# Layer 1's sparse-attention indexer with a narrow key projection and chunk-wise first products, the last norm by token halves, and one DMA sum fewer in the first unit

## The chip, the core and the metric

One core of one Trainium2 chip runs the whole program in one launch. The metric is the device time of the program in microseconds (us): the median of the runs shown. TensorE (PE in the rows) does the matrix products, VectorE (DVE), ScalarE (ACT) and GpSimd (POOL) the elementwise work, SyncE (SP) starts most loads.

## What is computed

The reference takes x, 512 tokens of 1024 features, through two layers, each of a half-step feed-forward, a mixer and another half-step feed-forward, all in fp32. The feed-forwards are SwiGLU with 2816 hidden features behind an RMS norm. Layer 0's mixer is a pair of state-space and mLSTM heads, which the change does not touch. Layer 1's mixer is sparse attention: an indexer scores each query against the keys, the 256 best of them stay, and attention runs on those. Cut to that:

```
q, k, v, qi, ki, wi = split(rms_norm(x) @ w_in)    # 1024 | 64 | 64 | 512 | 64 | 8 columns
q  = rope(rms_norm(q, 16 heads of 64));  k = rope(rms_norm(k))
qi = rope(qi, 8 heads of 64);            ki = rope(ki)
logits = einsum('thd,sd->tsh', qi, ki)
score  = einsum('tsh,th->ts', relu(logits), wi) * scale, -inf where s > t
sel    = top_k(score, 256)
o = softmax(q . k[sel] / 8, causal) @ v[sel];      x = x + o @ w_out
```

The first 128 tokens have at most 128 keys each, fewer than 256: of them only the index key ki is needed, not qi and wi.

## The kernel before, in words

**Products.** Every fp32 product is made of three matmuls: each operand is split into a high and a low part, and `mm3` (lines 276 to 282) adds high x high (L280), high x low (L281) and low x high (L282) into one PSUM bank. x lies in SBUF as 8 chunks of 128 features x 512 tokens. Ahead of a stage it is multiplied by the norm's gain and split into `xgn`: high part on ScalarE (L767), low part on VectorE (L770). The norm's scale by token, `rcol`, is applied only after the product, when ScalarE copies a bank out. `prep_later` does this for two chunks at a time; it also squares each chunk (ScalarE, L781) and adds the squares up (GpSimd, L476) into the tile `ssq`. The squares of the last two chunks are not added but stay separate summands. `settle_later` then has TensorE sum the squares over the features with one-column matmuls (`sums`, L411 to L415: 4 token blocks, each over all summands), VectorE scale and shift the result (L743), and GpSimd raise it to the power -1/2 (L745). A feed-forward also needs the scale along the rows: four transposes (`rows_of`, L435) and a copy (L749).

**Weights.** A weight block is loaded by SyncE into one of the 4 buffers `raw`, in turn, and formed into high and low parts in one of two ways (`both`). The plain way is `parts`: ScalarE copies the high part (L481) and VectorE subtracts for the low part (L483). The *summed* way has ScalarE write -raw (L510), then a DMA issued by GpSimd add raw to it in place (L511), and ScalarE write the high part (L512). For the sum to be the low part, -raw is written in the rounded type, so that adding raw leaves the rounding's rest.

**Order.** The feed-forwards' and the attention's work is entered into a plan: each step with its engine, an estimated duration, what it reads and writes. A list scheduler (`Plan.order`) takes at each point the step that can start earliest by the estimates, among equals the one that is due first, and the instructions of each engine are then pinned in that order. TensorE's steps carry a stream name ("filler", "index", "logits", "values"); within a stream they keep the order in which they were entered. One such plan holds FFN00, a second FFN01, FFN10, the attention and FFN11. Buffers that rotate are part of the plan: the n-th user of a tag with m buffers waits for the user m before it.

**The attention** (`attention`, from L1451). The indexer's weights are 584 columns: 512 of qi, 64 of ki, 8 of wi. They are taken in two halves (g = 0 and 1) of 292 columns, each in three blocks `iw` of chunks 0 to 2, 3 to 5 and 6 to 7, six blocks in all, loaded at L1467 and formed the plain way. So ki and wi lie in half 1. The products are made per token block b of 128 tokens and half g, each [128 tokens x 292], over 8 chunks, in the order (b, g) = (0,0), (1,0), (0,1), (1,1), (2,0), (3,0), (2,1), (3,1), in the two banks `gm` and `po` by turns. After the first product `settle_later` is entered, and from then on ScalarE copies each finished bank to `pr` with the scale (L1502). Then, per token block: rotary positions (`rope`, L1419 to 1423, VectorE), a doubled copy of the key (`twice`), transposes (`turned`), and for b = 1 to 3 the index logits (L1542), relu (L1548), weighted sum on VectorE (L1552, L1555), causal selection on GpSimd (L1557) and the top-k: 16 rounds of MAX8 and MATCH_REPLACE8 (L1760, L1761), which a constant of 60 keeps behind other work for b > 1. Behind the index products on TensorE come the key and value product, the queries (weights loaded at L1573, formed the summed way), then per token block the logits, softmax and values of the heads, in the order heads(0), heads(1), out(0), heads(2), heads(3), out(1, first 4 rows), out(1, last 4 rows). `out(half, ...)` is the output product for 256 tokens; after each chunk it is added to x (L476). In the last call `prep_later` is entered after every second chunk, for FFN11's norm, over all 512 tokens.

**The first unit.** A feed-forward unit has 4 weight blocks: gate and up, each in two interleaved halves (0, 1: gate; 2, 3: up). In the very first unit blocks 0 and 1 are formed the plain way and blocks 2 and 3 the summed way; the number is the last argument at the call in `ffn` (`2 * (1 - u) if first else 4`), where `u` is the unit: all four of unit 1 are summed.

## Time and profile before

| | us |
|---|---|
| median of 3 runs (lowest, highest) | 2037.05 (2032.81, 2038.75) |
| the profiled execution's own time | 2032.47 |
| its span in the profile | 2030.8 |
| mean granted TensorE clock over the span | 0.994 of full speed |
| TensorE busy | 1992.4 (98% of the span) |
| VectorE busy | 1581.0 (78%) |
| ScalarE busy | 1169.7 (58%) |
| GpSimd busy | 264.3 (13%) |

Times in rows count from the span's start. Matmuls are pipelined, so a TensorE row's duration overlaps the next row's; the distance of two starts is what one costs. The granted clock is a share of full speed, and its two levels are 1.00 (2.4 GHz) and 0.50 (1.2 GHz).

### The profile page before, as it was taken

The page shows a single profiled execution, that of the slowest core. Times are in us where ns is not written, and L with a number is a line of the kernel's source. Part 1 is how long each engine was busy: PE and PEld are TensorE (multiplying, and loading weights), DVE is VectorE, ACT ScalarE, POOL GpSimd, SP SyncE. Part 2 cuts the span into 40 slices and gives each one's busy share as a digit, 9 for nine tenths or more (in the row PEclk, how much of TensorE's full clock was granted, in tenths as well). Part 3 has the DMA queues.
Part 4 walks back from the last instruction along what each step waited for, and adds up shares of the span by engine and source line. Part 5 has one row for each costly group of instructions (what it writes and reads, how often), then busy time and mean ns, then how long its engine had stood idle before and what let it go on. Part 6 is the DMA issues. An engine that isn't in the chain of part 4 may idle for free.

```text
span 2030.8 us, 34575 instructions
## 1 busy us (share of the span) xinstructions
PE 1992.4 (98%) x13994; PEld 1808.0 (89%) x13994; DVE 1581.0 (78%) x2332; ACT 1169.7 (58%) x1709; POOL 264.3 (13%) x333
## 2 busy tenths in 40 slices
PE   8999999999999999999999999999998999999998
PEld 6999999887788888999998899999865667999998
DVE  6988888876537648988888998878588747988886
ACT  6666656442335434656566665656667544756565
POOL 1000001310001011010002000000215221101010
PEclk9999999999999999999999999999899999999999
DMA  8566665322221232666555366665653202566664
GB/s 220 143 161 153 167 153 141 115 83 74 72 84 63 74 102 65 167 159 164 156 151 140 99 172 157 167 152 141 175 124 90 63 11 73 148 161 161 155 168 114
DMA packets 211592, 260.74 MB, mean 128 GB/s; under 512 B 13804, under 2 KB 186984, under 8 KB 211432
## 3 DMA queue, kind: packets, MB, share of 16 engines
q1 hardware_dynamic: 190640, 185.58, 29.6%
q0 software_dynamic: 20592, 72.89, 19.1%
q8 instruction: 110, 1.80, 0.4%
q14 instruction: 50, 0.41, 0.1%
q10 hardware_dynamic: 200, 0.06, 0.0%
HBM read 183.53 MB, written 2.10 MB: 91 GB/s over the span
## 4 chain that ended last, share of the span: by engine, by line
PE 90%; DVE 5%; DMA 2%; issue 2%; ACT 1%; POOL 1%; ACTq 0%; DVEq 0%; POOLq 0%; SPq 0%
PE pA L281 10%; PE pA L280 10%; PE pA L282 10%; PE pD L281 5%; PE pD L280 5%; PE pD L282 5%; PE pB L281 3%; PE pB L280 3%; PE pB L282 3%; PE po L280 2%; PE po L282 2%; PE po L281 2%; PE pu L280 2%; PE pu L282 2%; PE ptok L280 1%
## 5 line engine op out<-in xcount | busy, mean ns | idle before, releaser
L483 DVE TENSOR_TENSOR form<-raw,form 128x1024 fp32r<-128x1024 f32 (+1 forms) x326 | 389.1, 1199 | 108.7 <-ACT form L481 107.9
L481 ACT ACTIVATE form<-raw 128x1024 fp32r<-128x1024 f32 (+1 forms) x326 | 333.4, 1027 | 178.8 <-DVE raw L476 129.4
L280 PE MATMUL pA<-xf,form 128*128 128x256 f32 x1152 | 322.2, 280 | 0.0
L281 PE MATMUL pA<-xf,form 128*128 128x256 f32 x1152 | 322.2, 280 | 0.0
L282 PE MATMUL pA<-xf,form 128*128 128x256 f32 x1152 | 322.0, 279 | 0.0
L476 DVE TENSOR_TENSOR raw<-raw 128x1024 f32<-128x1024 f32 (+2 forms) x241 | 283.8, 1181 | 12.7 <-DMA raw<-in_ffn_w_down 5.5
L511 POOL DMA_DIRECT2D form<-raw x137 | 117.9, 860 | 1206.0 <-ACT form L510 1145.9
L510 ACT ACTIVATE form<-raw 128x1024 fp32r<-128x1024 f32 (+1 forms) x137 | 141.3, 1031 | 142.5 <-PE pD L282 76.6
L280 PEld LDWEIGHTS pA<-xf,form 128*128 128x128 f32 x1152 | 216.5, 188 | 0.2
L281 PEld LDWEIGHTS pA<-xf,form 128*128 128x128 f32 x1152 | 216.4, 188 | 0.2
L282 PEld LDWEIGHTS pA<-xf,form 128*128 128x128 f32 x1152 | 216.3, 188 | 0.0
L281 PE MATMUL pA<-hid,form 128*128 128x256 f32 x704 | 198.6, 282 | 1.4 <-DVE hid L483 1.1
L280 PE MATMUL pA<-hid,form 128*128 128x256 f32 x704 | 198.1, 281 | 0.1
L282 PE MATMUL pA<-hid,form 128*128 128x256 f32 x704 | 196.9, 280 | 0.0
L281 PE MATMUL pD<-xf,form 128*128 128x256 f32 x576 | 161.2, 280 | 0.0
L280 PE MATMUL pD<-xf,form 128*128 128x256 f32 x576 | 161.2, 280 | 0.0
L282 PE MATMUL pD<-xf,form 128*128 128x256 f32 x576 | 161.1, 280 | 0.0
L476 DVE TENSOR_TENSOR ft<-ft 128x256 f32<-128x256 f32 (+2 forms) x288 | 146.3, 540 | 4.6 <-ACT ft L729 1.1
L512 ACT ACTIVATE form<-raw 128x1024 fp32r<-128x1024 f32 (+1 forms) x137 | 139.9, 1022 | 0.0
L281 PEld LDWEIGHTS pA<-hid,form 128*128 128x128 f32 x704 | 132.4, 188 | 3.2 <-DVE hid L483 3.1
L280 PEld LDWEIGHTS pA<-hid,form 128*128 128x128 f32 x704 | 132.3, 188 | 0.6 <-DVE ft L476 0.5
L282 PEld LDWEIGHTS pA<-hid,form 128*128 128x128 f32 x704 | 132.1, 188 | 0.0
(443 smaller groups left out, 5210.9 us busy)
## 6 DMA issues: line engine op xcount, KB each, us to landing
form<-raw POOLq DMA_DIRECT2D x121, 512.0 KB, 5.8
raw<-in_ffn_w_gate SPq DMA_DIRECT2D x88, 512.0 KB, 3.8
raw<-in_ffn_w_up SPq DMA_DIRECT2D x88, 512.0 KB, 3.7
raw<-in_ffn_w_down SPq DMA_DIRECT2D x64, 512.0 KB, 4.3
raw<-in_hy_w_in SPq DMA_DIRECT2D x44, 512.0 KB, 3.5
raw<-in_ffn_w_down SPq DMA_DIRECT2D x32, 384.0 KB, 3.4
raw<-in_hy_w_out SPq DMA_DIRECT2D x16, 512.0 KB, 3.3
form<-raw POOLq DMA_DIRECT2D x16, 384.0 KB, 4.1
```

The source lines that it names most:

```text
L280: mm(out, l[0], r[0], start=start, stop=False)
L281: mm(out, l[0], r[1], start=False, stop=False)
L282: mm(out, l[1], r[0], start=False, stop=stop)
L476: (self.p if pool else self.v)(n, lambda: e.tensor_tensor(out(), x(), y(), op=op), reads, writes)
L481: self.s(n, lambda: nc.scalar.activation(hi(), src(), AF.Copy), srck, hik)
L483: n, lambda: nc.vector.tensor_tensor(lo(), src(), hi().bitcast(F32), op=ALU.subtract), srck + hik, lok
L510: self.s(n, lambda: nc.scalar.activation(f()[:, 1], raw, AF.Copy, scale=-1.0), rawk, lok)
L511: self.plan.add("gpsimd", 0.85, lambda: nc.gpsimd.dma_start(f()[:, 1], raw, accum_op=ALU.add), rawk + lok, lok, 5.5)
L512: self.s(n, lambda: nc.scalar.activation(f()[:, 0], raw, AF.Copy), rawk, hik)
```

## The change

Three edits. (1) The indexer: product (0,0) is not made; product (0,1) is made only for the 64 columns of ki. The first four products, (0,1), (1,0), (1,1), (2,0), get a bank each and are made chunk by chunk group: chunks 0 to 3 of all four, then 6 and 7, then 4 and 5. `settle_later` and the four scaled copies come after all four. Then (2,1), (3,0), (3,1) follow one by one. The rotary scratch, the doubled key and the transposed queries share one 8 KB slot (`ri`, 2 buffers), likewise in `prepare` (`rq`, 2 buffers), and `pr` holds two token blocks per tile. (2) FFN11's norm: `prep_later` can do one half of the tokens. Chunks 0 to 3 of half 0 are done after out(0), chunks 0 to 3 of half 1 and chunks 4 to 7 whole after out(1). The squares lie in one tile of four. (3) The first unit forms block 2 the plain way too; only block 3 is summed.

```diff
-    def prep_later(self, which, k, last, squares=True):
+    def prep_later(self, which, k, last, squares=True, half=None):
...
-        if k == 0:
+        if k == 0 and not half:
...
+            squares4 = Lazy(lambda: self.tmp.tile([P, 4, T], F32, name="ssq", tag="ssq", bufs=1))
+            self.sqs = [lambda i=i: squares4()[:, i] for i in range(4)]
...
+        halves = (0, 1) if half is None else (half,)
+        cols = slice(halves[0] * H, halves[-1] * H + H)
+        n = cols.stop - cols.start
...
-                    made = self.unit(raws, stream, bool(first) and not u, 2 * (1 - u) if first else 4)
+                    made = self.unit(raws, stream, bool(first) and not u, 3 * (1 - u) if first else 4)
...
-        for b0 in (0, 2):
-            for g in range(2):
-                for b in (b0, b0 + 1):
-                    ps, psk = self.bank(("gm", "po")[b % 2])
-                    for g2, k, f, fk, j in iw:
...
-                    if self.pending == 2:
-                        self.settle_later()
-                        rcol = self.rcol
+        def indexer(jobs, ks):
+            for b, g, (ps, psk) in jobs:
+                cols = slice(0 if b else KI - N1, N1 if b else KI - N1 + 64)
+                tok = slice(b * P, (b + 1) * P)
+                for k, f, fk, j in ((k, f, fk, j) for k0 in ks for g2, k, f, fk, j in iw if (g2, k) == (g, k0)):
+                    product(
+                        lambda ps=ps, cols=cols: ps()[:, cols], psk, lambda k=k, tok=tok: [xg[i][k][:, tok] for i in range(2)], xgk(k),
+                        lambda f=f, j=j, cols=cols: [f()[:, i, j, cols] for i in range(2)], [(*fk, 0), (*fk, 1)],
+                        cols.stop - cols.start, k == 0, k == 5,
+                    )
...
+        jobs = [(0, 1, self.bank("gm")), (1, 0, self.bank("po")), (1, 1, self.bank("lg")), (2, 0, self.bank("lg"))]
+        for ks in ((0, 1, 2, 3), (6, 7), (4, 5)):
+            indexer(jobs, ks)
+        self.settle_later()
+        rcol = self.rcol
+        scaled(jobs)
+        for b, g, tag in ((2, 1, "gm"), (3, 0, "po"), (3, 1, "gm")):
+            jobs = [(b, g, self.bank(tag))]
+            indexer(jobs, (0, 1, 2, 3, 6, 7, 4, 5))
+            scaled(jobs)
...
+            ri, rik = self.spot("ri", (4 * T,), 2)
+            self.rope(x, xk, n, cos, sin, [tk(0), tk(1)], ri, rik)
...
-                if last and k % 2:
-                    self.prep_later(nxt, k - 1, k == KC - 1)
+                if last and k % 2 and (half or k < 4):
+                    self.prep_later(nxt, k - 1, k == KC - 1, half=half if k < 4 else None)
...
-        out(0, range(KC))
+        out(0, range(KC), True)
```

## Rows read from the trace of the kernel before

**Rows 1.** The page's parts 1 and 4: busy time of each engine (share of the span) and instructions; and the chain of work that ended last, shares of the span by engine.

```profile
PE 1992.4 (98%) x13994; PEld 1808.0 (89%) x13994; DVE 1581.0 (78%) x2332; ACT 1169.7 (58%) x1709; POOL 264.3 (13%) x333
...
PE 90%; DVE 5%; DMA 2%; issue 2%; ACT 1%; POOL 1%; ACTq 0%; DVEq 0%; POOLq 0%; SPq 0%
```

**Rows 2.** One answer of the windows view. Columns: the stretch (us from the span's start), its length; then busy us (instructions) of PE, PEld, DVE, ACT and POOL; the granted TensorE clock as a share of full speed; the busy share of the DMA engines; GB/s. The first three stretches are the indexer's products, the fourth row is the attention from the first top-k round to the last, the last two the start of FFN11.

```profile
1435.20:1440.20 5.00, 2.09 (x12) 1.39 (x11) 4.97 (x6) 4.08 (x8) 2.93 (x3) 1.00 0.01 4
1440.20:1453.80 13.60, 12.87 (x52) 12.18 (x53) 8.71 (x15) 5.23 (x10) 1.22 (x2) 0.50 0.57 176
1453.80:1478.40 24.60, 24.60 (x177) 22.61 (x177) 5.12 (x13) 16.04 (x29) 5.57 (x7) 1.00 0.94 212
...
1484.40:1608.50 124.10, 115.63 (x591) 74.81 (x590) 111.79 (x341) 83.69 (x187) 43.00 (x62) 0.99 0.40 90
...
1664.00:1689.30 25.30, 22.03 (x161) 20.18 (x160) 19.94 (x25) 14.40 (x21) 7.70 (x5) 1.00 0.34 105
1689.30:1696.20 6.90, 6.90 (x23) 5.84 (x23) 0.24 (x2) 0.00 (x0) 1.03 (x1) 0.51 0.00 0
```

**Rows 3.** The timeline of TensorE in the index stage: start us, duration us, engine, line, operation, out<-in, shape, count, and in brackets the idle time before it and what ended it.

```profile
1440.83 0.61 PE L281 MATMUL gm<-iw,xgn 128*128 128x292 f32 x1 [1.53 <-DVE iw L483]
...
1445.30 0.42 PE L414 MATMUL pssq<-raw,ssq 128*128 128x1 f32 x2
...
1450.28 0.59 PE L280 MATMUL po<-iw,xgn 128*128 128x292 f32 x1
...
1454.37 0.30 PE L280 MATMUL po<-iw,xgn 128*128 128x292 f32 x1
...
1454.77 0.30 PE L280 MATMUL po<-iw,xgn 128*128 128x292 f32 x1
```

**Rows 4.** What feeds the index stage, 1428 to 1448: the timelines of VectorE, GpSimd (POOL), ScalarE (ACT) and SyncE's queue (SPq), and last the DMA issues of the same stretch (KB each, median us from issue to landing).

```profile
1430.23 2.16 DVE L483 TENSOR_TENSOR iw<-raw,iw 128x876 fp32r<-128x876 f32 x1
...
1434.01 0.74 DVE L770 SCALAR_TENSOR_TENSOR xgn<-raw,xgn 128x512 fp32r<-128x512 f32 x1
...
1437.26 1.46 DVE L770 SCALAR_TENSOR_TENSOR xgn<-raw,xgn 128x512 fp32r<-128x512 f32 x1
...
1438.64 2.14 DVE L483 TENSOR_TENSOR iw<-raw,iw 128x876 fp32r<-128x876 f32 x1
...
1444.69 2.71 DVE L483 TENSOR_TENSOR iw<-raw,iw 128x876 fp32r<-128x876 f32 x3
...
1436.89 2.96 POOL L476 TENSOR_TENSOR ssq<-ssq,sq 128x512 f32<-128x512 f32 x2 [3.35 <-ACT sq L781]
...
1443.59 0.69 ACT L481 ACTIVATE iw<-raw 128x584 fp32r<-128x584 f32 x1 [0.78 <-DMA raw<-in_sa_w_in]
...
1429.41 11.80 SPq L1467 DMA_DIRECT2D raw<-in_sa_w_in  x3
...
raw<-in_sa_w_in SPq DMA_DIRECT2D x2, 438.0 KB, 3.3
```

**Rows 5.** The timelines of GpSimd, ScalarE and VectorE between the sums and the first rotary operation of token block 1: the power that makes the scale, the first scaled copy out of PSUM, the first rotary product.

```profile
1450.69 1.14 POOL L745 TENSOR_TENSOR raw<-raw 128x4 f32<-128x4 f32 x1 [10.80 <-DVE raw L743]
...
1451.87 0.50 ACT L1502 ACTIVATE pr<-gm,raw 128x292 f32<-128x292 f32 x1 [7.59 <-POOL raw L745]
...
1462.34 0.76 DVE L1419 TENSOR_TENSOR rot<-pr,raw 128x576 f32<-128x576 f32 x1 [2.50 <-ACT pr L1502]
```

**Rows 6.** The instructions on the tile of the scores: the top-k's maxima by shape (mean ns of each), with the first start and the last end.

```profile
L1760 DVE MAX8 keep<-keep x48: 418/555/697, 1484.4 to 1606.6; 128x8 f32<-128x256 f32 x16, 128x8 f32<-128x384 f32 x16, 128x8 f32<-128x512 f32 x16
```

**Rows 7.** The timelines around the starts of FFN11 (first four rows, TensorE and VectorE) and of FFN10 (last two: the first of its sums, and the first matmul behind them).

```profile
1676.19 0.50 PE L281 MATMUL pg<-xgn,form 128*128 128x512 f32 x1 [0.77 <-DVE xgn L770]
...
1680.99 0.50 PE L281 MATMUL pg<-xgn,form 128*128 128x512 f32 x1 [1.42 <-DVE xgn L770]
...
1688.03 0.38 PE L414 MATMUL pssq<-raw,sq 128*128 128x1 f32 x2 [1.00 <-ACT sq L781]
...
1676.39 1.64 DVE L770 SCALAR_TENSOR_TENSOR xgn<-raw,xgn 128x512 fp32r<-128x512 f32 x1
...
1104.83 0.28 PE L414 MATMUL pssq<-raw,ssq 128*128 128x1 f32 x2
...
1107.42 0.48 PE L280 MATMUL pu<-xgn,form 128*128 128x512 f32 x1
```

**Rows 8.** The costliest groups by line and shape: two groups of half-width (256-column) instructions; busy us, mean ns | idle us before them.

```profile
L476 DVE TENSOR_TENSOR ft<-ft 128x256 f32<-128x256 f32 x176 | 68.1, 422 | 2.5
...
L1322 ACT ACTIVATE hsq<-pn 128x256 f32<-128x256 f32 x16 | 6.1, 381 | 0.0
```

**Rows 9.** The first unit of FFN00: timelines of GpSimd (the two DMA sums' issues), VectorE and TensorE, and last, from the page's costliest groups, the low parts of weight blocks.

```profile
12.45 1.01 POOL L511 DMA_DIRECT2D form<-raw  x1 [9.51 <-ACT form L510]
16.77 0.86 POOL L511 DMA_DIRECT2D form<-raw  x1 [3.32 <-ACT form L510]
...
17.64 0.69 DVE L375 COPY raw<-pxt 128x512 f32<-128x512 f32 x1 [2.04 <-PE pxt L368]
...
25.07 0.50 PE L282 MATMUL pu<-xgn,form 128*128 128x512 f32 x1 [2.93 <-DMA form<-raw]
...
28.39 0.39 PE L282 MATMUL pu<-xgn,form 128*128 128x512 f32 x1
...
L483 DVE TENSOR_TENSOR form<-raw,form 128x1024 fp32r<-128x1024 f32 (+1 forms) x326 | 389.1, 1199 | 108.7 <-ACT form L481 107.9
```

More of the change, by code (lines that the diff above doesn't have):

```diff
@@ L412, in sums @@
         for b in range(NB):
-            for i, x in enumerate(parts):
+            some = [x for x, b0 in parts if b >= b0]
+            for i, x in enumerate(some):
                 self.nc.tensor.matmul(
-                    ps[:, b : b + 1], x[:, b * P : (b + 1) * P], self.ones1, start=i == 0, stop=i == len(parts) - 1
+                    ps[:, b : b + 1], x[:, b * P : (b + 1) * P], self.ones1, start=i == 0, stop=i == len(some) - 1
                 )
@@ L422, in rms_col @@
         ps = self.aux("pssq", (T,))
-        self.sums(ps, ssq)
+        self.sums(ps, [(x, 0) for x in ssq])
         ms, rcol = (self.cols[:, self.turn, i] for i in range(2))
@@ L442, in settle @@
         if self.pending == 2:
[L443 removed]
+            self.rcol = self.rms_col([x() for x, _ in self.ssqs], D)
         if self.pending == 1:
@@ L772, in low @@
                     self.mark = ins
-            self.v(T, low, self.xk(j) + hik, lok)
+            self.v(n, low, self.xk(j, halves) + hik, lok)
             if not squares:
@@ L1411, in rope_tables, with rope @@
         return tab, part
[L1413 removed]
+    def rope(self, x, xk, n, cos, sin, reads, t, tk):
         v = self.nc.vector
[L1416 to L1418 removed]
+        k1, k2 = (*tk, 0), (*tk, 1)
+        p1, p2 = (lambda i=i: t()[:, i * n * 64 : (i + 1) * n * 64].rearrange("p (n d) -> p n d", d=64) for i in range(2))
         self.v(n * 64, lambda: v.tensor_tensor(p2(), x(), sin(), op=ALU.mult), [xk, *reads, ("raw", "sum")], [k2])
@@ L1440, in turned, with twice @@
         return ps, psk
-    def twice(self, n, x, xk):
-        t, tk = self.spot("two", (NB, 2, 64), 2)
+    def twice(self, n, x, xk, t, tk):
+        t = lambda t=t: t().rearrange("p (n a d) -> p n a d", a=2, d=64)
         self.s(n * P, lambda: self.nc.scalar.activation(
@@ L1458, in attention @@
         QI0, KI, WI, N1 = 1152, 512, 576, 292
-        iw = []
-        for c0, floor in ((QI0, plan.floor), (QI0 + N1, len(plan.steps) - 1)):
-            plan.floor = floor
+        iw, last = [], len(plan.steps) - 1
+        for c0 in (QI0, QI0 + N1):
             for k0, k1 in ((0, 3), (3, 6), (6, 8)):
+                if k1 == KC:
+                    plan.floor = last
                 n = k1 - k0
@@ L1469, in attention @@
                 f = lambda f=f: f()[:, :, 0 : 3 * N1].rearrange("p i (k n) -> p i k n", k=3)
-                hi, lo = (lambda f=f, n=n, j=j: f()[:, j, 0:n] for j in range(2))
-                self.parts(n * N1, hi, lo, lambda raw=raw: raw, [(*fk, 0)], [(*fk, 1)], [("raw", i)])
+                self.both(lambda f=f, n=n: f()[:, :, 0:n], [(*fk, 0)], [(*fk, 1)], raw, [("raw", i)], False)
                 iw += [(c0 != QI0, k, f, fk, k - k0) for k in range(k0, k1)]
-        pr = [self.spot("pr", (2 * T,), NB) for _ in range(NB)]
+        keep, kept = self.spot("keep", (4 * T,), 1)
+        two = [self.spot("pr", (2, 2 * T), 2) for _ in range(2)]
+        pr = [(lambda t=two[b // 2][0], i=b % 2: t()[:, i], (*two[b // 2][1], b % 2)) for b in range(NB)]
         keys, keysk = self.spot("keys", (4, T), 1)
@@ new lines, in scaled @@
+        def scaled(jobs):
+            for b, g, (ps, psk) in jobs:
+                cols = slice(0 if b else KI - N1, N1 if b else KI - N1 + 64)
+                self.s(cols.stop - cols.start, lambda b=b, g=g, ps=ps, cols=cols: act(
+                    pr[b][0]()[:, g * N1 + cols.start : g * N1 + cols.stop], ps()[:, cols], AF.Copy, scale=rcol[:, b : b + 1]
+                ), [psk, "rcol"], [pr[b][1]])
+        jobs = [(0, 1, self.bank("gm")), (1, 0, self.bank("po")), (1, 1, self.bank("lg")), (2, 0, self.bank("lg"))]
@@ L1600, in attention @@
         for k in range(KC):
-            product(ps, psk, lambda k=k: [f()[:, i, k] for i in range(2)], fk, lambda k=k: [xg[i][k] for i in range(2)], xgk(k), T, k)
+            product(ps, psk, lambda k=k: [f()[:, i, k] for i in range(2)], fk, lambda k=k: [xg[i][k] for i in range(2)], xgk(k), T, k == 0, k == KC - 1)
         kvf, kvfk = lambda: keys()[:, 3], (*keysk, 3)
```

69 lines of the change are left out of this document (29 added, 40 removed).

## Prediction

> **What bounds the kernel now.** I read the page's busy row and its chain of waits first: TensorE is busy 98% of the span and makes 90% of the chain [rows 1]. A change can shorten this kernel only where TensorE does less, waits less, or runs at a higher granted clock, so I cut the stretches that the change touches into a table by stage [rows 2]. Two stand out. The indexer's products run from 1435.2 to 1478.4, 43.2 us; in the first 5.0 TensorE is busy for 2.09, and in the next 13.6 it is granted the lower of its two levels. The last feed-forward's start, 1664.0 to 1696.2, has 3.3 us of idle time and then 6.9 at the lower level. Between them, 1484.4 to 1608.5, TensorE is busy 115.6 of 124.1 and VectorE 111.8, so there neither has much room. Third come the single instructions at those places: TensorE's waits and prices in the index stage [rows 3], what feeds it [rows 4], the scale behind the products and the rotary work [rows 5], the top-k [rows 6], the starts of two feed-forwards [rows 7], and the first unit [rows 9].
>
> **Part 1, the indexer.** A full product is 8 triples of 292 columns. Two triples start 0.40 us apart at the full clock [rows 3], so one product is 3.2 us and the eight are 25.6. The 43.2 then divide into 25.6 of products; 2.6 for the 24 one-column matmuls of the sums (the same 24 take 1104.83 to 1107.42 at FFN10's start, 0.108 each [rows 7]); 2.9 idle in the first 5.0 (and another 1.53 behind them for the second block's low part [rows 3]); 6.4 lost to the clock (half of the 12.87 busy at 0.50 [rows 2]); and the remaining 5.7 for the index transposes and logits between them.
> - *Removed and narrowed.* Two full products go (6.4). For the 64-column one that is left no row exists. Bounds: 24 matmuls in proportion to columns, 0.7; no gain at all, 3.2. I take the one-column price, 24 x 0.108 = 2.6, because 64 columns are nearer to 1 than to 292. Products: 19.2 + 2.6 = 21.8, so 3.8 less.
> - The Trainium skill ("TensorE: Matmul & The Clock Gate", the section on the back-to-back issue gap) spaces load and matmul pairs of 128 columns some 81 ns apart; by it the narrow product would be an estimated 1.9 us and the sum 0.7 lower.
> - *Waits at the start.* The first job is now the narrow one, and it needs the second weight half: the fourth and fifth blocks. The fifth is loaded into the buffer that the first block frees when its low part is done, 1430.23 + 2.16 = 1432.4; a load takes 3.3 [rows 4], so it lands about 1435.7, and its high part (under 1 us) and low part (2.1 beside GpSimd's additions) end about 1438.7. TensorE idles from 1435.2 to 1438.7 but for nine narrow triples (1.0): 2.5, against 2.9 before. Bounds 1.0 (VectorE takes the low part uncontended) and 5 (it stands behind other low parts).
> - *A new wait in the middle.* Chunks 6 and 7 of the second half are in the sixth block, whose load waits for the second block's low part (1438.64 + 2.14) and lands at about 1443.5 [rows 4]. The four jobs' first chunks are done at about 1443.8, and that block's low part a little over 2 us later. If the planner advances the second block (chunk 3 now needs it early), nothing is left. Bounds 0 and 2.7; I take 1.4.
> - *A wait that loses its cover.* The scale (tensor_scalar, GpSimd's power) is ready 1.6 us after the sums: they end at 1450.28 and the first scaled copy starts at 1451.87 [rows 3, 5]. TensorE ran the next job meanwhile. Now the sums stand behind four jobs in four banks, and the next job needs a bank that a scaled copy must free, with that copy's 0.5: 2.0 uncovered, bounds 1.6 and 2.6. Behind it only the three last jobs are queued; the weights' transfers run on.
> - *The clock.* The half-clock stretch follows the starved 5 us. The new start is starved about as much, so I take half of the 6.4 as lost, 3.2, bounds 0 and 6.4.
>
> Sum: 21.8 + 2.6 + 2.5 + 1.4 + 2.0 + 3.2 + index work 5.0 (one block fewer to turn off the path) = 38.5, so the stage is 4.7 shorter; bounds 0 and 10. The rotary work of block 1 starts at 1462.34 now [rows 5]; it must wait for all four jobs, the sums and the scale, which end near 1458, so VectorE's chain to the top-k moves 3 to 4 earlier, less than TensorE. The top-k itself is unchanged (48 MAX8 [rows 6] and their replacements). As both engines are near full in 1484.4 to 1608.5, I carry 4.5 through. The tiles repacked into 8 KB slots add waits of a third user on the first; they lie behind logits that are done far ahead, and cost nothing as long as the logits stay ahead of the rotary work two heads on.
>
> **Part 2, the norm by halves.** Four chunks of half 0 move out of the stretch after the last output products into the attention. Added there: 8 ACT operations of 0.38 and 4 of VectorE at 0.42 (nearest half-width rows [rows 8]), 3 GpSimd additions. ACT has room; VectorE's 1.7 lie among its 10% of slack, so I take 0.5 of them on the path, bounds 0 and 3.6 (each instruction twice as long beside GpSimd). Removed at the end: as much ACT and VectorE work ahead of FFN11's first products. TensorE's waits there, 0.77 and 1.42, are for low parts, one of which took 1.64 [rows 7]; two us less work ahead of them leaves 0.2, so 2.0 gained. The sums' stand of 1.00 is for the last squares and stays. Then 6.9 us at half clock cost 3.4. FFN10's start has the same 24 sums and goes on at full speed behind them: its next triple starts 2.59 after them. So with shorter waits the dip may go; I take half, 1.7. Part 2: -3.7 and +0.5, bounds -6 and +3.6.
>
> A moved addition could hurt VectorE: a low part takes 0.74 alone and 1.46 beside GpSimd's additions [rows 4]. [...]
>
> **Part 3, the first unit.** TensorE stands 2.93 us for the third block's DMA sum, which was issued at 12.45 and ends at 25.0 [rows 9]. That block's low part becomes a VectorE subtraction of 1.2, put where VectorE waits 2.04 for TensorE's transposes; without that cover it costs 1.2. Then the fourth block's sum is needed about 24.9. It is now the only one in its queue, so I let it land where the first did, 25.0. Gain 2.5; bounds 0 (it still lands at 28, where its third matmul needs it now) and 2.9.
>
> **Sum.** -4.5 + 0.5 - 3.7 - 2.5 = -10.2 on the profiled execution's 2032.5: 2022.3. The median of the runs shown is 4.6 above that execution, and I forecast against the median: 2026.9, say 2027.
>
> **Rivals.**
> - *A, the attention keeps its end.* VectorE is busy 111.8 of 124.1 there, and the top-k ends at 1606.6 [rows 6], just before the last heads need it. If what sets the end is VectorE's queue rather than TensorE's, part 1 gives about 1 and only parts 2 and 3 remain, with half of each: 2037 - 1 - 3 = 2033. For it: the VectorE share [rows 2]. Against: rotary work and selection also start earlier.
> - *B, slower: the half clock fills the index stage.* Four jobs that wait chunk by chunk, then one-column sums, then an uncovered wait could keep TensorE at the lower level for the whole stage: products 43.6, sums 5.2, index work 10, waits 5.9, together 64.7 against 43.2, +21.5; less 5.7 from the rest, 2053. It decides from the point where more than about 28 us run at half clock (13.6 now): each us at half clock loses 0.5, and the edits' other gain is some 7.4 here and 5.7 elsewhere. For it: such a stretch exists now, right behind a starved start. Against: from 1453.8 the same kind of products runs at 1.00 [rows 2]. The Trainium skill ("TensorE: Matmul & The Clock Gate", the clock-gate section) has the low level as the default that only sustained work lifts, which leans this way.
> - *C, larger.* No clock loss in the index stage (-3.2), no wait for the sixth block (-1.4), the dip before FFN11 wholly gone (-1.7), and 5 of the 8.5 us that TensorE idles in the attention closed by the new order: about 2016.
> - *D, no narrower in time.* The 64-column product costs 3.2: only 0.6 worse, inside the forecast.
>
> **How the numbers follow.** Forecast with D 0.57 (its own range 2020 to 2031), A 0.20, C 0.15, B 0.08. What these runs can tell from no change is 0.3%, about 6 us: faster is under 2031, slower over 2043. Faster: the forecast and C, with a little of A: 0.74. Same: most of A: 0.18. Slower: B: 0.08. The range, 2012 to 2037, takes in C with its bounds below and A up to no gain.
>
> **What would show it.** In the changed profile: narrow triples about 0.32 apart and 56 product triples in place of 64; the sums behind four jobs with an idle TensorE of about 2 behind them; the index stage near 38.5 and the first MAX8 3 to 4 earlier; a stand under 0.3 at FFN11's first low parts; no wait for the third block near 22, and none over 0.5 for the fourth. A top-k that ends no earlier would show A; a granted clock of 0.50 over more than 28 us, B. If the index stage ends earlier by 4 and the span doesn't follow, my carrying-through was wrong.

## The result and the profile after

The changed kernel takes 2026.7 us in the median of 6 runs (2020.96 to 2028.19), the kernel before 2034.8 in 6 (2032.81 to 2038.75): the ratio on record is 0.9946, 95% interval 0.9931 to 0.9962, some 11 us of 2036 (the quotient of these two medians alone would be 0.9960, or 8.1 us; all microseconds of gain below are worked out from the ratios on record in the same way). Measured twice more, the same kernel stood at 0.9931 (0.9918 to 0.9944) and 0.9942 (0.9924 to 0.9960). The forecast was 2027. The total came out, but partly by luck: the indexer gave more than its term and the first unit less.

The profiled execution took 2021.98 us (span 2020.3), 10.5 less than that of before. The page's busy row and chain of waits of the changed kernel, which answer to [rows 1]:

```profile
PE 1986.4 (98%) x13970; PEld 1802.2 (89%) x13970; DVE 1581.2 (78%) x2337; ACT 1169.9 (58%) x1715; POOL 264.9 (13%) x335
...
PE 85%; DVE 5%; DMA 5%; issue 2%; ACT 1%; POOL 1%; SPq 0%; ACTq 0%; POOLq 0%; DVEq 0%
```

TensorE is busy 6.0 us less and the span is 10.5 shorter: the other 4.5 are waits. The windows view by stage, as [rows 2] (length, then busy us of PE, PEld, DVE, ACT, POOL; granted clock; DMA share; GB/s). The first five rows are the index stage, then the attention up to its last output products, then from those to a late product of FFN11's first unit:

```profile
1438.32:1442.01 3.69, 0.30 (x2) 0.18 (x1) 3.69 (x4) 1.54 (x5) 1.12 (x1) 1.00 0.15 19
1442.01:1446.46 4.45, 4.45 (x23) 4.45 (x24) 4.45 (x5) 3.10 (x6) 2.86 (x2) 0.62 0.97 302
1446.46:1455.90 9.44, 9.44 (x74) 9.44 (x74) 4.16 (x8) 7.91 (x10) 3.86 (x6) 1.00 0.84 188
1455.90:1458.88 2.98, 2.73 (x26) 2.64 (x24) 0.16 (x1) 1.10 (x2) 0.00 (x0) 1.00 1.06 198
1458.88:1472.88 14.00, 13.39 (x87) 12.04 (x87) 6.01 (x14) 9.92 (x20) 3.07 (x4) 0.88 0.92 239
1472.88:1640.29 167.41, 159.32 (x828) 100.76 (x827) 136.44 (x403) 113.28 (x253) 61.32 (x90) 0.99 0.34 78
1640.29:1687.98 47.69, 46.55 (x303) 39.87 (x302) 22.08 (x36) 15.61 (x26) 7.73 (x6) 0.93 0.19 56
```

Cut at the same places, the kernel before has:

```profile
1435.26:1478.43 43.17, 39.52 (x240) 36.15 (x239) 18.77 (x33) 25.38 (x44) 9.74 (x11) 0.84 0.71 177
1478.43:1647.21 168.78, 156.21 (x816) 99.09 (x815) 134.59 (x401) 109.99 (x244) 57.39 (x84) 0.99 0.33 76
1647.21:1698.15 50.94, 47.36 (x306) 40.08 (x306) 25.52 (x35) 17.39 (x26) 11.27 (x10) 0.93 0.17 52
```

Read three things. The index stage fell from 43.2 to 34.6. The attention's length hardly changed, 168.8 to 167.4, although TensorE is busy 3.1 longer in it (some of the index transposes and logits now lie there): its idle time fell from 12.6 to 8.1. And FFN11's start fell from 50.9 to 47.7 with 2.4 less idle, at the same clock of 0.93. Ahead of the index stage the changed kernel is 3.1 *later* (1438.32 against 1435.26), which hides as much of the gain in this pair of executions. Of that, 1.6 came at FFN10's sums, where the granted clock over 1100 to 1125 is 1.00 in the execution of before and 0.93 here. It is not the change's: in two more profiled executions of the changed kernel it is 1.00 and 0.80, and the index stage starts at 1436.0 and 1442.4.

Within the index stage, TensorE's timeline of the changed kernel, as [rows 3]:

```profile
1442.01 0.30 PE L281 MATMUL gm<-iw,xgn 128*128 128x64 f32 x1 [3.40 <-DVE iw L485]
...
1442.26 0.28 PE L280 MATMUL gm<-iw,xgn 128*128 128x64 f32 x1
...
1442.59 0.28 PE L280 MATMUL gm<-iw,xgn 128*128 128x64 f32 x1
...
1455.90 2.73 PE L416 MATMUL pssq<-raw,ssq 128*128 128x1 f32 x24
1458.88 0.40 PE L280 MATMUL gm<-iw,xgn 128*128 128x292 f32 x1 [0.26 <-DVE raw L745]
```

A narrow triple takes 0.33 (0.40 at 292 columns [rows 3]). TensorE stands 3.40 for a low part at the start, and behind the sums only 0.26. The fifth product starts at 1458.88, *before* the first scaled copy below empties a bank: it had a bank of its own. Its short stand is for VectorE's reading of the sums. ScalarE's and VectorE's timelines and the top-k's tile, as [rows 5, 6]:

```profile
1459.98 0.31 ACT L1516 ACTIVATE pr<-gm,raw 128x64 f32<-128x64 f32 x1 [2.98 <-POOL raw L747]
```

```profile
1440.90 2.41 DVE L485 TENSOR_TENSOR iw<-raw,iw 128x876 fp32r<-128x876 f32 x3
...
1461.51 0.76 DVE L1429 TENSOR_TENSOR ri<-pr,raw 128x576 f32<-128x576 f32 x1 [0.49 <-ACT pr L1516]
```

```profile
L1791 DVE MAX8 keep<-keep x48: 415/555/696, 1479.5 to 1604.0; 128x8 f32<-128x256 f32 x16, 128x8 f32<-128x384 f32 x16, 128x8 f32<-128x512 f32 x16
```

The times in such a row are those of the first and of the last start. The first MAX8 stands 41.1 us behind the start of the index stage, against 49.1 before. At FFN11's start the two stands for low parts of [rows 7] are gone; the sums still wait 0.87, and they run at half clock:

```profile
1677.36 4.15 PE L416 MATMUL pssq<-raw,ssq 128*128 128x1 f32 x24 [0.87 <-POOL ssq L478]
```

In the first unit (TensorE, then GpSimd) the stand of 2.93 [rows 9] is gone too, but the start is slower and the one sum that is left is waited for. It was issued at 15.42 and ends at 28.4:

```profile
14.49 0.80 PE L281 MATMUL pg<-xgn,form 128*128 128x512 f32 x1 [0.72 <-DVE xgn L781]
28.40 0.50 PE L282 MATMUL pu<-xgn,form 128*128 128x512 f32 x1 [1.15 <-DMA form<-raw]
```

```profile
15.42 1.01 POOL L513 DMA_DIRECT2D form<-raw  x1 [12.48 <-ACT form L512]
```

### The profile page after: what moved, and what is told of

It reads as the page before. It is cut to its first block, busy times and chain, and to the rows that moved or that the text cites. A ratio compares the mean times of both kernels' runs of the same rounds, so it can differ in the third digit from the quotient of the medians.

```text
span 2020.3 us, 34527 instructions
## 1 busy us (share of the span) xinstructions
PE 1986.4 (98%) x13970; PEld 1802.2 (89%) x13970; DVE 1581.2 (78%) x2337; ACT 1169.9 (58%) x1715; POOL 264.9 (13%) x335
## 4 chain that ended last, share of the span: by engine, by line
PE 85%; DVE 5%; DMA 5%; issue 2%; ACT 1%; POOL 1%; SPq 0%; ACTq 0%; POOLq 0%; DVEq 0%
PE pA L281 9%; PE pA L280 9%; PE pA L282 9%; PE pD L281 5%; PE pD L280 5%; PE pD L282 5%; PE pB L281 2%; PE pB L280 2%; PE pB L282 2%; DMA form<-raw 2%; PE po L280 2%; PE po L282 2%; PE po L281 2%; PE ptok L280 1%; PE pu L280 1%
```

## The experiments

Since executions of one kernel start the index stage more than 6 us apart (1436.0 and 1442.4 above), I read each trace from distances inside it. All are in this table, in us: **stage**, from the first index product to the first key-and-value product; **MAX8**, from the first index product to the first top-k round; **idle**, TensorE's idle time from the stage's end to the first product of the last output (length less busy time in the windows view); **to out**, from the first index product to that last output; **FFN11**, from there to the same late product of its first unit in every kernel. **to out** less **stage** is the length of the attention; each distance is from one execution.

| kernel | ratio to before (95%) | stage | MAX8 | idle | to out | FFN11 |
|---|---|---|---|---|---|---|
| before | 1 | 43.2 | 49.1 | 12.6 | 212.0 | 50.9 |
| changed, three executions | 0.9946, 0.9931, 0.9942 | 34.6, 35.3, 36.8 | 41.1, 41.9, 43.4 | 8.1, 9.0, 8.5 | 202.0, 203.4, 206.0 | 47.7, 47.6, 46.0 |
| indexer alone | 0.9961 (0.9948 to 0.9973) | 37.0 | 43.6 | 8.6 | 205.7 | 50.5 |
| norm by halves alone | 0.9986 (0.9978 to 0.9995) | 43.9 | 50.6 | 11.3 | 212.6 | 47.7 |
| first unit alone | 0.9996 (0.9986 to 1.0006) | 43.2 | 49.3 | 11.5 | 211.2 | 49.3 |
| less work, old order | 0.9968 (0.9957 to 0.9979) | 39.2 | 45.9 | 8.7 | 205.9 | 50.6 |
| new order, full work | 0.9974 (0.9964 to 0.9985) | 39.4 | 45.3 | 9.0 | 206.6 | 50.5 |
| same bank | 0.9962 (0.9949 to 0.9975) | 35.1 | 47.4 | 11.0 | 208.7 | 46.1 |
| late settle | 0.9958 (0.9943 to 0.9973) | 36.2 | 42.7 | 9.1 | 204.6 | 46.0 |
| three products ahead | 0.9949 (0.9933 to 0.9965) | 33.1 | 36.5 | 8.5 | 202.0 | 47.6 |
| late top-k | 0.9965 (0.9952 to 0.9977) | 35.5 | 47.8 | 12.8 | 209.4 | 47.9 |
| no sum in the first unit | 0.9944 (0.9929 to 0.9959) | 37.3 | 43.8 | 9.0 | 205.6 | 47.6 |

**The three parts, each alone, and the whole again.** The indexer alone is the changed kernel with

```diff
-                if last and k % 2 and (half or k < 4):
-                    self.prep_later(nxt, k - 1, k == KC - 1, half=half if k < 4 else None)
+                if last and k % 2:
+                    self.prep_later(nxt, k - 1, k == KC - 1)
...
-        out(0, range(KC), True)
+        out(0, range(KC))
...
-    made = self.unit(raws, stream, bool(first) and not u, 3 * (1 - u) if first else 4)
+    made = self.unit(raws, stream, bool(first) and not u, 2 * (1 - u) if first else 4)
```

> The indexer's edit alone; the norm of the last feed-forward whole and two DMA sums in the first unit, as before. Theory (read from the two traces): the index stage and the attention give nearly all of the gain, 9 to 10 us, ratio about 0.9953, because TensorE never waits for the scale (its next product has a bank of its own) and loses little to the clock. Rival (the recorded sum): 4.5 us, ratio 0.9978, with the rest of the measured gain from the other two edits. The first index product's start should stand behind FFN10's end as before, with no shift ahead of it beyond 1 us.

Measured: 0.9961, 7.9 us. The interval shuts out the recorded 4.5 (0.9978) and takes in the 9 to 10. The theory's "little to the clock" does not hold in its trace: the granted clock over the stage is 0.82 there, 0.84 before. That nothing shifts ahead of the index stage was wrong for the profiled execution: the stage starts at 1442.1 there, and the clock at FFN10's sums is 0.93 again. The norm alone is the kernel before with the change's `sums` and `prep_later`, and

```diff
-        out(0, range(KC))
+        out(0, range(KC), True)
...
-                if last and k % 2:
-                    self.prep_later(nxt, k - 1, k == KC - 1)
+                if last and k % 2 and (half or k < 4):
+                    self.prep_later(nxt, k - 1, k == KC - 1, half=half if k < 4 else None)
```

> The last norm by token halves alone. Theory: TensorE's two waits for low parts at FFN11's start (0.77 and 1.42) go, the half clock around the sums stays: about 2 to 3 us, ratio 0.9986. Recorded sum: 3.2 us with half of the clock loss back, 0.9984. Rival: the moved work makes the top-k's chain later by up to 3.6 us and the total is unchanged or slower, 1.000 to 1.001.

Measured: 0.9986, 2.9 us. In its trace FFN11's start is 47.7, as in the changed kernel; from the index stage's start to the last output it takes 212.6 against 212.0. The rival falls. The recorded 3.2 (0.9984) lies in the interval as well; for the theory speaks that the granted clock over FFN11's start is 0.93 in this trace as in that of before. The first unit alone:

```diff
-    made = self.unit(raws, stream, bool(first) and not u, 2 * (1 - u) if first else 4)
+    made = self.unit(raws, stream, bool(first) and not u, 3 * (1 - u) if first else 4)
```

> One DMA sum fewer in the first unit alone. Theory (from the two traces): nothing, ratio 1.000 within 0.0007, since the one sum that is left lands as late as the second one did (28 us) and its block is the one that waits. Recorded sum: 2.5 us faster, 0.9988. Rival: the edit makes the start later, and the 2.9 us that the changed kernel had lost by FFN10's end are its price: 1.0014.

Measured: 0.9996, 0.8 us and not told apart from nothing; the rival of 2.9 us lost is shut out, the recorded 2.5 (0.9988) lies just inside the interval. The runs' granted clock is 0.9930 on average against 0.9924 in the runs of before beside them, which is an estimated 1.2 us and more than the 0.8. The trace says why the 2.5 did not come. TensorE stands for the last sum, and then near 104 us in FFN00, where the new plan has VectorE take up a weight block before its load is there. TensorE's timeline at the two places, VectorE's ahead of the second, and last the product of the third row as it stands in the kernel before:

```profile
28.04 0.50 PE L282 MATMUL pu<-xgn,form 128*128 128x512 f32 x1 [1.68 <-DMA form<-raw]
...
103.88 0.38 PE L280 MATMUL pA<-hid,form 128*128 128x256 f32 x1 [0.49 <-ACT hid L481]
...
104.96 0.39 PE L281 MATMUL pA<-hid,form 128*128 128x256 f32 x1 [0.70 <-DVE hid L483]
```

```profile
97.35 1.23 DVE L476 TENSOR_TENSOR raw<-raw 128x1024 f32<-128x1024 f32 x1 [2.54 <-DMA raw<-in_ffn_w_down]
```

```profile
104.40 0.28 PE L281 MATMUL pA<-hid,form 128*128 128x256 f32 x1
```

That product comes 0.56 later than before: by 105 us the edit has gained nothing in this trace. All nine profiled executions that form the third block the plain way stand near 104 us (1.1 to 1.3 together), none of the five others. The three gains, 7.9 + 2.9 + 0.8 = 11.6, add up to the whole (11.0, 14.0 and 11.8 in its three measurements).

> The changed kernel once more, unaltered. Theory: ratio 0.9946 again, and the 2.9 us by which the profiled execution of the changed kernel was late at FFN10's end (a late weight load near 96 and near 984 us, a half-clock stretch at FFN10's sums near 1109) do not all come back in this profile: they belong to the execution. Rival: the same three losses stand at the same places, because the order of the work makes them.

Measured: 0.9931. At FFN10's sums TensorE's clock is 1.00 this time, and the index stage starts at 1436.0. But the late load near 96 is here again and, as just seen, goes with the first unit's edit; the one near 984 is here too (0.96), but not in the third execution of the same kernel. So each side is right on a part: of the 2.9, some 1.2 is the edit's and the rest the execution's.

**Work or order?** Two kernels split the indexer's edit, both with the other two edits undone. One makes the seven products one by one:

```diff
-        jobs = [(0, 1, self.bank("gm")), (1, 0, self.bank("po")), (1, 1, self.bank("lg")), (2, 0, self.bank("lg"))]
-        for ks in ((0, 1, 2, 3), (6, 7), (4, 5)):
-            indexer(jobs, ks)
-        self.settle_later()
...
+        for b, g, tag in ((1, 0, "po"), (0, 1, "gm"), (1, 1, "po"), (2, 0, "gm"), (2, 1, "po"), (3, 0, "gm"), (3, 1, "po")):
+            jobs = [(b, g, self.bank(tag))]
+            indexer(jobs, range(KC))
+            if first:
+                self.settle_later()
...
```

> The indexer's edit without its order: one product dropped and the key's narrowed to 64 columns as in the change, but the seven are made one by one, all chunks of each, in before's manner, with the sums behind the first; the other two edits undone. Theory (half of the index gain is work, half is order): 3.5 to 4.5 us faster than before, ratio 0.998; TensorE starved in the first 5 us and at half clock for about 13 us as before. Rival (all of it is work): 8 us, as with the index edit alone, 0.996. Recorded prices: 3.8 us for the work.

The other keeps the new order and makes all eight at full width:

```diff
-                cols = slice(0 if b else KI - N1, N1 if b else KI - N1 + 64)
+                cols = slice(0, N1)
...
-        for b, g, tag in ((2, 1, "gm"), (3, 0, "po"), (3, 1, "gm")):
+        for b, g, tag in ((0, 0, "po"), (2, 1, "gm"), (3, 0, "po"), (3, 1, "gm")):
```

> The indexer's order without its saving: all eight products of 292 columns (the key's product at full width, the one for block 0's unused columns added behind the four), the first four chunk by chunk with the sums behind them; the other two edits undone. Theory: the order by itself gives 3.5 to 4.5 us (less half clock, no stand between chunks), ratio 0.998. Rival (the order gives nothing, the saving all): 1.000; rival of the recorded sum: a wait of 2.0 behind the sums eats part of it, 0.9992.

Measured: 0.9968 (6.5 us) and 0.9974 (5.3 us). Both lie above the expected 3.5 to 4.5, but both intervals still take in 4.5, and that of less work its rival's 8 too. Together they are 11.8, where the indexer with both halves has 7.9; the difference of 3.9 is about what the three intervals allow (2.1 to 2.5 us to each side), so the totals do not show that the halves overlap. In the traces the stages are 39.2 and 39.4, about 4 shorter each, and in both the attention's idle time has *already* fallen to 8.7 and 9.0. The windows view of the less-work kernel, stage and attention:

```profile
1440.48:1479.68 39.20, 35.13 (x212) 32.54 (x210) 20.77 (x36) 21.50 (x37) 8.41 (x9) 0.83 0.67 168
1479.68:1646.36 166.68, 158.01 (x824) 101.07 (x823) 134.68 (x397) 112.83 (x247) 61.52 (x88) 0.98 0.37 83
```

and of the one with the new order:

```profile
1438.39:1477.80 39.41, 33.81 (x234) 31.54 (x235) 17.92 (x31) 25.73 (x42) 12.02 (x13) 0.96 0.92 220
1477.80:1645.02 167.22, 158.26 (x825) 100.72 (x823) 134.03 (x398) 108.70 (x242) 58.01 (x85) 0.98 0.30 68
```

So the two gains in the stage add up: 4.0 + 3.8 = 7.8, where the indexer alone is 6.2 shorter and the changed kernel 6.4 to 8.6. The attention is 2.1 and 1.6 shorter than before in these two executions (166.7 and 167.2 against 168.8); with both halves together it is not (below). In the execution of the new order the clock over the stage is 0.96 against 0.83 with less work, and the idle time there is 5.6, more than the 3.7 of before. That the order gains by the clock is not shown: the indexer alone makes its products in the same order and has 0.82.

**The bank.** To see what the wait behind the sums costs where it does exist, the last three products are put into the banks of the first three:

```diff
-        for b, g, tag in ((2, 1, "gm"), (3, 0, "po"), (3, 1, "gm")):
-            jobs = [(b, g, self.bank(tag))]
+        banks = [bank for _, _, bank in jobs]
+        for (b, g), bank in zip(((2, 1), (3, 0), (3, 1)), banks):
+            jobs = [(b, g, bank)]
```

> The changed kernel, but the fifth product (block 2, half 1) is made in the very bank of the key's product, and the sixth and seventh in those of the second and third, so that each must wait for a scaled copy. Theory: TensorE then stands about 1.6 to 2.3 us behind the sums instead of 0.26, and the kernel is that much slower than the changed one (ratio to before about 0.9950 against 0.994). Rival: the stand is there but the attention takes it up, and the total does not move.

TensorE does stand, 1.73, and for the scaled copy:

```profile
1464.03 0.61 PE L280 MATMUL gm<-iw,xgn 128*128 128x292 f32 x1 [1.73 <-ACT pr L1516]
```

The ratio is 0.9962, about 4 us worse than the changed kernel. How much of that is the stand's price is not shown: the 2 us that were expected (0.9950) lie just inside the interval, and the runs' granted clock is 0.9922 on average against 0.9930 to 0.9942 in the three measurements of the changed kernel, an estimated 2 to 4 us. In the trace the stage is not longer (35.1, with fewer index transposes in it); the attention is, 173.6, of which some 2 to 3 us are more idle time:

```profile
1440.88:1476.02 35.14, 30.04 (x199) 29.83 (x199) 17.58 (x28) 22.23 (x38) 10.67 (x11) 0.85 0.79 196
1476.02:1649.58 173.56, 162.58 (x836) 103.55 (x835) 137.68 (x405) 115.18 (x257) 64.02 (x90) 0.97 0.34 76
```

Its first MAX8 comes 47.4 behind the index start, 12.3 behind the end of the stage, where the changed kernel has 6.6. That is more than the stand. The index logits take their banks by the name `lg`, which the seventh product now holds too, and they start 36.6 behind the index start, where they do so 30.3 behind it in the changed kernel (first row same bank, second row changed):

```profile
1477.49 0.70 PE L1571 MATMUL lg<-keys,ri 64*128 64x256 f32 x4
```

```profile
1468.60 0.70 PE L1570 MATMUL lg<-keys,ri 64*128 64x256 f32 x4
```

So this edit does more than make one wait. It pointed to the chain from the scale through rotary work and index logits to the first top-k round, and two kernels move that round with TensorE's work as it is: one enters it later, one brings the scale earlier.

```diff
+                if (b, i) == (2, 1):
+                    plan.add("vector", 0.0, lambda: None, [sk], [maskk[1]])
+                    self.topk(mask[1], maskk[1], lambda r: m8()[:, 0, r % 2], 2 * P)
...
             plan.later = 60.0 * (b > 1)
-            self.topk(sc, sk, lambda r, b=b: m8()[:, b - 1, r % 2], n)
+            if b > 1:
+                self.topk(sc, sk, lambda r, b=b: m8()[:, b - 1, r % 2], n)
```

> The changed kernel, but the first top-k (token block 1) is entered behind the scores of four heads of block 2, so that on VectorE it starts 4 to 7 us later; nothing else is changed, TensorE's index products stay. Theory (the first top-k round sets the end): the end comes 4 to 6 us later than the changed kernel's, ratio to it 1.002 to 1.003. Rival (VectorE only needs its work done, in whatever order): within 1 us of the changed kernel.

```diff
-        jobs = [(0, 1, self.bank("gm")), (1, 0, self.bank("po")), (1, 1, self.bank("lg")), (2, 0, self.bank("lg"))]
+        jobs = [(0, 1, self.bank("gm")), (1, 0, self.bank("po")), (1, 1, self.bank("lg"))]
...
-        for b, g, tag in ((2, 1, "gm"), (3, 0, "po"), (3, 1, "gm")):
+        for b, g, tag in ((2, 0, "gm"), (2, 1, "po"), (3, 0, "gm"), (3, 1, "po")):
```

> The changed kernel, but only three products, (0,1), (1,0), (1,1), are made chunk by chunk ahead of the sums; (2,0) comes behind them. Same work on TensorE. In all traces so far the attention's last output products start 160 to 163 us behind the first top-k round, while the distance from the end of the index products varies from 167 to 174. Theory (the chain scale, rotary work, index logits, first top-k round sets the attention's end): the sums and the scale come 3 us earlier, the first MAX8 1.5 to 3 earlier, and the end follows by as much against the changed kernel of this same call. Rival (TensorE's position sets it): no change beyond 1 us, since its work and its waits stay.

> The changed kernel, unaltered, as the measure for the other three of this call: ratio to before 0.993 to 0.995.

Beside these two the changed kernel is at 0.9942. The late top-k is at 0.9965, 4.7 us worse, as the theory said (the two intervals overlap by 0.0008; the granted clock of the runs is 0.9928 and 0.9930, so it is not that). Its stage is as short as the changed kernel's, its first round comes 12.3 behind the end of the stage, and the idle time is 12.8. Its windows row for the attention and its top-k row:

```profile
1473.63:1647.56 173.93, 161.17 (x829) 101.34 (x827) 136.52 (x403) 112.99 (x253) 63.23 (x90) 0.98 0.33 75
```

```profile
L1795 DVE MAX8 keep<-keep x48: 414/556/696, 1486.0 to 1608.6; 128x8 f32<-128x256 f32 x16, 128x8 f32<-128x384 f32 x16, 128x8 f32<-128x512 f32 x16
```

The early one is at 0.9949: no gain is seen, though its first MAX8 comes 36.5 behind the index start, 5 to 7 earlier, and 3.4 behind the end of its stage:

```profile
1475.05:1643.90 168.85, 160.38 (x819) 102.38 (x819) 135.75 (x399) 111.97 (x249) 62.20 (x89) 0.97 0.32 74
```

```profile
L1791 DVE MAX8 keep<-keep x48: 418/556/695, 1478.4 to 1606.6; 128x8 f32<-128x256 f32 x16, 128x8 f32<-128x384 f32 x16, 128x8 f32<-128x512 f32 x16
```

So the theory holds on one side; on the other nothing was seen of the 1.5 to 3 us, though the two intervals do not shut them out, and the attention of this execution was granted 0.97, the changed kernel's 0.98 to 0.99. The attention's length (to out less stage) sums it up: 166.7 to 169.3 in every kernel whose first top-k round comes up to 6.7 behind the end of its stage, 173.6 and 173.9 in the two where it comes 12.3 behind. A round that is held back holds the end up, and one that comes 3 us sooner than in the changed kernel was not seen to help.

The kernel before is not such a case. Its first round comes 5.9 behind its stage, and its attention is 168.8 long. Its larger idle time has in part another cause: 1.3 of the 12.6 stand ahead of the first MAX8, for ScalarE's doubled key, as do 2.1 with the norm alone and 1.5 with the first unit alone.

```profile
1481.32 0.33 PE L1433 MATMUL pq<-raw,two 128*128 128x128 f32 x1 [1.33 <-ACT two L1445]
```

```profile
1484.37:1647.21 162.84, 151.60 (x794) 95.59 (x793) 128.93 (x390) 104.22 (x233) 55.63 (x82) 0.99 0.31 69
```

```profile
1487.86:1649.87 162.01, 152.84 (x798) 96.55 (x797) 131.77 (x394) 107.47 (x242) 61.13 (x88) 0.99 0.31 71
```

From the first MAX8 to the last output TensorE idles 11.2 in the kernel before (first windows row) and 9.2 with the norm alone (second), whose first round is the latest of all, 50.6 behind the index start. The changed kernel has 8.1 to 9.0. So the idle time by itself does not show that a late round costs time; the late top-k does.

**FFN11's sums later, and no sum at the start.** Two tries to take more, both on the changed kernel. The first:

```diff
-    made = self.unit(raws, stream, bool(first) and not u, 3 * (1 - u) if first else 4)
+    made = self.unit(raws, stream, not u and (bool(first) or self.stage == "ffn11"), 3 * (1 - u) if first else 4)
```

> The changed kernel, but FFN11's first unit makes its sums after the third weight block's first products instead of after the second's, as the very first unit does. Theory: the 0.87 us that TensorE stands for GpSimd's last addition goes; whether the half clock around the sums goes with it tells if that stand brings it: with it 4 us faster than the changed kernel, without it 0.9. Rival: the row of scales comes later, the products' copies wait for it, 1 to 2 us slower.

Measured: 0.9958, not faster. The sums wait 0.88 for GpSimd's last addition as before: with the output products woven in, that addition came as late as the sums at either place. The clock over FFN11's start is 0.96, but it is 0.96 or 0.97 in three executions without this edit and 0.93 in others, so the try says nothing on the dip. The second:

```diff
-    made = self.unit(raws, stream, bool(first) and not u, 3 * (1 - u) if first else 4)
+    made = self.unit(raws, stream, bool(first) and not u, 4 * (1 - u) if first else 4)
```

> The changed kernel with no DMA sum at all in the first unit: the fourth block, too, gets its low part from VectorE. Theory: TensorE's stand for the last sum (1.0 to 2.4 us in the traces with one sum) goes, and the first unit, from its first product to the ninth triple of its second half, falls from 21.2 to about 20 us; on the total about 1, at the edge of what the runs can tell. Rival: ScalarE and VectorE are full there and the norm's work comes later, so that nothing is gained.

Measured: 0.9944, where the changed kernel beside it has 0.9942. In the trace the first unit, from its first product to the ninth gate triple, takes 19.7, without a stand for a sum, against 21.1 to 21.5 in the three executions of the changed kernel. The 1.5 is seen in the trace and too small for the totals. No version tried beats the changed kernel by more than the measurement can tell.

## Why the prediction was right, point by point

- **The bound** held: TensorE is busy 98% in both, and what was gained is TensorE's work, waits and clock.
- **Part 1, the stage** was put at 38.5; it is 34.6, 35.3 and 36.8 in the three executions. By terms, in the first: the narrow product 24 x 0.11 = 2.7 (put at 2.6). The Trainium skill's spacing ("TensorE: Matmul & The Clock Gate", back-to-back issue gap, some 81 ns) would have made it an estimated 1.9; the trace has 111 ns, and the measurement decides. The wait at the start 3.4 (2.5, within its bounds), but not for the fifth block's load: VectorE was late with the low parts, the case that I had as the upper bound. The wait for the sixth block 0 (1.4). The clock: two stretches at half speed, (1 - 0.62) x 4.45 + (1 - 0.88) x 14.00 = 3.4 (3.2). The rest of the miss, some 2 us, is index work that slid out of the stage into the attention (about 2.9 were left in the stage, where I took 5.0). Two slips in the reading did not reach the sum: the "nine narrow triples" at the start are nine matmuls, three triples; and the stand of 1.53 lies for the most part inside the 2.9 of idle time, not behind it.
- **The step that failed, "A wait that loses its cover"**: 2.0, with bounds of 1.6 to 2.6, measured 0.26. I read one bank per name in the code; the product behind the sums got another bank and needed no copy. The experiment with the same bank shows that the size of the wait was right where it exists (1.73); what it costs in the end stays open, since that edit moved the index logits too.
- **The other step that failed, the lead of the chain**: I had the first MAX8 "3 to 4 earlier, less than TensorE". It came 8.0, 7.2 and 5.8 earlier, and the stage's end 8.6, 7.9 and 6.4: one followed the other. "I carry 4.5 through" held in kind, since the attention added nothing and took nothing: 168.4 on average in six executions of the indexer's edit (the changed kernel's three, the indexer alone, the late settle and no sum in the first unit), 168.5 in the three without it. What was off was the size of the lead. The distance from the index start to the last output is 204.5 in the six against 211.9 in the three, 7.4 shorter, where I had 4.0 with the moved norm, and the stage makes 7.2 of it. That the work which slid into the attention did not lengthen it I had not foreseen. Why the length stays the same there, with TensorE idle for 8 to 9 us, is shown only in part: a late first round lengthens it.
- **Part 2** was put at -3.7 and +0.5. FFN11's start is 3.2 shorter: 2.4 of idle time (2.0 expected), and the clock, of which I had taken half as won, gave little: 0.93 in the changed kernel's first two executions as before, 0.96 in the third. The work moved into the attention costs nothing that can be seen (212.6 against 212.0, with the index stage 0.7 longer). The moved additions fell beside the last top-k, so that their price for VectorE can be read. GpSimd's and VectorE's timelines of the changed kernel:

```profile
1598.47 1.60 POOL L478 TENSOR_TENSOR ssq<-ssq 128x256 f32<-128x256 f32 x2
1602.85 0.73 POOL L478 TENSOR_TENSOR ssq<-ssq 128x256 f32<-128x256 f32 x1 [2.78 <-ACT ssq L792]
```

```profile
1597.41 0.68 DVE L1791 MAX8 keep<-keep 128x8 f32<-128x512 f32 x1
...
1599.40 0.68 DVE L1791 MAX8 keep<-keep 128x8 f32<-128x512 f32 x1
...
1600.20 0.68 DVE L1792 MATCH_REPLACE8 keep<-keep 128x512 f32<-128x512 f32 x1
...
1602.17 0.69 DVE L1791 MAX8 keep<-keep 128x8 f32<-128x512 f32 x1
1602.89 0.09 DVE L1792 MATCH_VALUE_LOAD keep<-keep 128x8 f32 x1
1602.97 0.67 DVE L1792 MATCH_REPLACE8 keep<-keep 128x512 f32<-128x512 f32 x1
1603.56 0.47 DVE L781 SCALAR_TENSOR_TENSOR xgn<-raw,xgn 128x256 fp32r<-128x256 f32 x1
```

  The rounds beside an addition (1599.40, 1602.97) take what the others take, 0.68 and 0.67. The Trainium skill ("SBUF — State Buffer", who interferes with whom) says that a VectorE instruction with at most one input in SBUF, outside its two-port modes, does not contend with GpSimd. For these two operations the trace agrees, 0.68 and 0.67 beside an addition and 0.68 to 0.69 without one.
- **Part 3**, -2.5, was too large: 0.8 in the totals, not told apart from nothing. "I let it land where the first did" failed, and its lower bound was what came: alone in its queue the sum took 13.0 us from issue to TensorE's going on (15.42 to 28.40), no less than the first of the two before (12.45 to 25.07 [rows 9]), and it was issued 3 us later than that one. TensorE stood 1.15 for it, where I had put up to 0.5 as the sign of being right. And I priced the edit as if the plan around it stayed: the re-planned FFN00 gives some 1.2 back near 104 us.
- **The rivals.** A did not come: the attention's end moved by as much as the stage's and the first round did. B (whose turning point by its own terms is some 27 us, not 28: the moved norm's 0.5 was taken off twice), the half clock through the index stage, did not come: 3.4 us were lost to it in the first execution, and the stage's granted clock is 0.90, 0.90 and 0.81 in the three, against 0.84 before. C was near in the fall of the attention's idle time (5 of the 8.5; 3.6 to 4.5 of 12.6 came), but work that slid in filled it, and C needed the clock as well, which it did not get. D fell, if barely: the narrow product is 0.5 shorter than a full one's 3.2.
- **The sum** was right by luck, because the indexer's miss (7.4 instead of 4.0), the first unit's (0.8 instead of 2.5) and FFN11's (3.2 instead of 3.7) partly cancel: 11.4 against 10.2. The total alone would have shown none of the steps that failed.

## What to carry to other kernels

Where a long serial chain on one engine (here the top-k) runs beside a full engine, measure how far behind the full engine's work it starts, from a fixed point of the same trace: here 6 us behind did no harm, 12 us behind cost about 5, and 3 us behind was not seen to gain. Price the stretch by its whole length, too, and not by idle time alone: work that slides across the cut looks like a gain on one side. Before pricing a wait for a buffer, look at which buffer the next instruction takes. And test the halves of an edit apart and together, with intervals that can tell their sum from the whole; here they could not.

## What was not expected of the hardware

- The DMA sum of 512 KB that TensorE stands for in the first unit was used 12.6 us after its issue with a second one behind it and 13.0 us after it alone; in the changed kernel the next one, 512 KB too and issued at 26.77, landed 6.5 us after its issue, and one of 384 KB near 1427 took 5.8 (the DMA views of 26 to 28 and of 1424 to 1440). What holds the early ones up was not tried.
- The clock at the same place of the same program differs between executions: over 1100 to 1125 the granted clock is 0.93, 1.00 and 0.80 in three executions of the changed kernel, though TensorE stands there for the same two low parts, 1.01 and 0.72, 1.02 and 0.74, 1.01 and 0.72. Over the index stage it is 0.90, 0.90 and 0.81. A term of the sum that is a share of such a stretch can only be given as a range.
